# A two-layer decoder trunk on one core: every operation recorded first, then emitted in an order worked out from a table of the engines

## The chip, the core and the metric

The kernel runs on one core of a Trainium2 chip. The metric is device microseconds of one launch. A core has five engines with instruction streams of their own: TensorE (PE in the profile, its weight loads PEld), VectorE (DVE), ScalarE (ACT), GpSimd (POOL) and SyncE (SP), which here issues DMAs only; ACT issues some DMAs as well. Every engine carries out its own stream in the order in which the program was written, and waits on semaphores for the others. The question of this case is that order.

## The reference, cut to what matters

The input x has 2048 positions of 1024 features, in float32. What is computed:

```python
h = rmsnorm(x, norm_a)
b, c, xin, g = split(h @ w_in_a, 4)                    # 1024 x 4096
x = x + (b * conv3(c * xin) * silu(g)) @ w_out_a       # causal, three taps
k, v = split(rmsnorm(x, norm_kv) @ w_kv, 2)            # 8 heads of 64
q, g = split(rmsnorm(x, norm_b) @ w_in_b, 2)
for each block of 128 queries:                         # stick-breaking attention
    z = q @ k.T / 8
    rev = reversed cumulative sum over the keys of log_sigmoid(-z), strictly causal
    o = exp(z + rev) @ v
x = x + (o * silu(g)) @ w_out_b
out = rmsnorm(x, norm_f)
```

## The kernel before

**Tiling.** The 2048 positions are four chunks of 512 columns, and they are held reversed, so that the cumulative sum runs forward along the free axis and chunk c attends to chunks c, c-1, ..., 0. A product in (nearly) float32 is three matmuls in float32r: operands are split into a high and a low part (`split`, L163: a copy on ACT and a subtraction on DVE, or on POOL), and `mm3` (L192) does high x high, high x low, low x high for each of the 8 blocks of 128 input features. One output tile of 128 x 512 is therefore 24 matmuls into one bank of PSUM; the pool `lin` has two such banks.

**Stages.** `mixer_in` (L273) makes the gates C, X, B, G of the first layer for a chunk; `proj_out` (L374) its output projection; `proj_k`, `proj_q`, `proj_v`, `proj_g` (L407 to L441) the projections of the second layer; `out_b` and `out_norm` (L583, L605) the last projection and the last norm, and `out_b_last` (L623) both for chunk 3. I call all of this the filler: it is dense PE work. The other kind is `attention` (L477), by chunk and head. For a block of 128 queries (`qi`) and 512 keys it does two matmuls z (L498, L499), two sigmoids on ACT into R and w (L501, L503), on POOL a copy of the carry into R's first column, or the causal mask (L511, L507), on DVE a scan along the keys into R (L512) and the product w*R (L516); then for each 128 keys (`kb`) it transposes four blocks of w on PE into `wt` (L524), splits them into `wth` on ACT and `wtl` on DVE (L531), and adds both to `av` by two matmuls (L533, L534). Attention is what loads DVE.

**What sets the order.** Each stage is a generator that yields an estimate of its PE work. `merge` (L700) advances two or three of them in proportion to their totals (with exponents S2, S3, S4, S7 that bend the proportion), and so gives the order in which the operations are written. The framework (`schedule_with_timeline_sim`, L778) then orders them anew on each engine by a simulation of its own. In the last quarter of the program (`fine` on, L746) every third matmul of the filler has an order-only dependence on the `av` matmul of nine key blocks ago (L199 to L201), which paces the filler by the attention.

**Names that the prediction uses.** Chunk 3 is the last, with heads 3_0 to 3_7 and four blocks of keys each. `sga` is a tile of silu(g) that L556 loads over SP's queue; `gated` (L559) multiplies it with a head pair's output `ot` and splits the product into `og`, which `out_b` consumes. For the last pair `ot` is still in SBUF, and the product is L566. `pol` are the 24 matmuls (L645) that come after it. `hl` is a single buffer through which the splits of k, q and v go to DRAM.

Of the kernel before, what the change touches and what calls it, by code (L numbers as in the profile page):

```python
# [1 line left out]

# [12 lines left out]
P = 128  # L15
S = 2048
D = 1024
NH = 8
# [12 lines left out]
GRP, GRY, SLACK = 3, 6, 8  # L31
PACE = mybir.DependencyInfo(mybir.DependencyClass.NoSync, mybir.DependencyReason.DATA)
# [4 lines left out]
EPS = 1e-6  # L37

# [7 lines left out]
def kernel(  # L46
# [15 lines left out]
    nc = tc.nc  # L62

    const = ctx.enter_context(tc.tile_pool(name="const", bufs=1))
    psum = ctx.enter_context(tc.tile_pool(name="psum", bufs=2, space=bass.MemoryType.PSUM))
    dram = ctx.enter_context(tc.tile_pool(name="dram", bufs=1, space=bass.MemoryType.DRAM))
    sb = ctx.enter_context(tc.tile_pool(name="sb", bufs=2))

    ident = const.tile([P, P], F32, name="ident")
    make_identity(nc, ident)  # L70
# [23 lines left out]
    v_d = [dram.tile([P, 4, NH, 2, 64], F32, name=f"v_d_{c}") for c in range(NCH)]  # L94
    xn_d = [[dram.tile([P, 2, CH], F32, name=f"xn_d_{c}_{k}") for k in range(KD)] for c in range(NCH - 2)]
    sg_d = [[dram.tile([P, CH], F32, name=f"sg_d_{c}_{h}") for h in range(NH // 2)] for c in range(NCH)]
    og_d = [[dram.tile([P, CH], F32, name=f"og_d_{c}_{h}") for h in range(NH // 2)] for c in range(NCH)]
# [91 lines left out]
    anchors = []  # L189
    fine = [24, False]  # L190

    def mm3(ps, wts, a, kt=KD):  # L192

        hi, lo = wts[:, 0], wts[:, 1]
        n = 0
        for k in range(kt):
            for w, m in ((hi, 0), (hi, 1), (lo, 0)):
                ins = nc.tensor.matmul(ps, w[:, k, :], a[k][:, m, :], start=n == 0, stop=n == 3 * kt - 1)  # L198
# [4 lines left out]
                if n % fine[0] == 0 and n < 3 * kt:  # L203
                    yield MM * fine[0]

    def rest(n):
        return MM * (n - (n - 1) // fine[0] * fine[0])
# [219 lines left out]
    def proj_v(c, vb):  # L427
# [10 lines left out]
        nc.sync.dma_start(out=v_d[c][:, :, 2 * vb:2 * vb + 2, :, :], in_=vt.bitcast(F32))  # L438
# [38 lines left out]
    def attention(c, h, ot):  # L477
# [8 lines left out]
        for kc in range(c, -1, -1):  # L486
# [5 lines left out]
            nc.scalar.dma_start(out=vt.bitcast(F32), in_=v_d[kc][:, :, h, :, :])  # L492
# [26 lines left out]
            for kb in range(3, -1, -1):  # L519
# [14 lines left out]
                ins = nc.tensor.matmul(av[:, 0:n], vs, wl[:, 0:n], start=False, stop=final)  # L534
                anchors.append(ins)
# [47 lines left out]
    def out_b(c, obs):  # L583
# [3 lines left out]
        for ob in obs:  # L587
# [3 lines left out]
            x = ld512(f"x1o_{c}_{ob}")  # L591
# [191 lines left out]
```

## Time and profile before

| | |
|---|---|
| three runs | 1887.19, 1879.34, 1883.08 us; median 1883.08 |
| the profiled execution | 1879.53 us, of it 1877.6 us from the first to the last instruction |
| PE | 1778.2 us busy (95%), 8312 instructions |
| DVE | 1242.5 us (66%), 1830 |
| ACT, POOL | 773.3 us (41%), 432.9 us (23%) |
| DMA | 464.63 MB, mean 247 GB/s |

PE's shares are of time in which some matmul was under way; matmuls overlap in the pipe, so the mean duration of one (399 ns for a 512-wide one) is longer than the distance of two. That distance is read from a stretch in which PE never idles, as stretch over count. The clock that PE was granted is in the column PEclk (1.00 is full).

### The profile page before, as it was taken

Reading aid. Unit: us, or ns where it says so; the run is one execution under the profiler, and the core shown is the slowest. Engines: PE = TensorE matmul, PEld = TensorE weight load, DVE = VectorE, ACT = ScalarE, POOL = GpSimd, SP = SyncE. Lnnn points to the kernel's source line nnn. Section 1 sums busy time; section 2 is a strip of 40 time slices with the busy share of each in tenths; the row PEclk is TensorE's granted clock in tenths of the full one; section 3 lists DMA queues with packets and bytes.
Section 4 is the critical chain, followed back from the end, with each engine's and each line's share of the span. In section 5 each row is a group of like instructions: output and inputs, shape, how many; then the busy total and the mean of one; then the engine's idle time right before and its main releaser. Section 6 shows DMA issues by size and latency. Waiting matters only on the chain.

```text
span 1877.6 us, 24847 instructions
## 1 busy us (share of the span) xinstructions
PE 1778.2 (95%) x8312; PEld 1448.5 (77%) x8312; DVE 1242.5 (66%) x1830; ACT 773.3 (41%) x1493; POOL 432.9 (23%) x814
## 2 busy tenths in 40 slices
PE   7999999999999999999999999999998998987884
PEld 5888888888778878887888888888776886865573
DVE  7766643554243364478784477787868888799874
ACT  6423311231132142345443344454535555566542
POOL 5000000101021032032221122232223212357533
PEclk9999999999999999999999999999999999998887
DMA  9999995687978697867687765666586666878663
GB/s 295 326 297 326 330 308 168 213 311 277 337 253 285 219 324 264 286 220 250 208 253 237 257 201 187 196 200 214 186 291 202 212 205 233 275 235 261 224 203 131
DMA packets 240783, 464.63 MB, mean 247 GB/s; under 512 B 18704, under 2 KB 133392, under 8 KB 216080
## 3 DMA queue, kind: packets, MB, share of 16 engines
q1 hardware_dynamic: 180576, 404.28, 63.5%
q10 hardware_dynamic: 59920, 58.74, 11.0%
q8 instruction: 66, 1.08, 0.2%
q14 instruction: 61, 0.50, 0.1%
q0 software_dynamic: 160, 0.02, 0.1%
HBM read 326.92 MB, written 136.05 MB: 247 GB/s over the span
## 4 chain that ended last, share of the span: by engine, by line
PE 76%; DMA 9%; DVE 7%; issue 3%; ACT 2%; POOL 2%; SPq 0%; ACTq 0%; POOLq 0%; DVEq 0%
PE pG L198 9%; PE pB L198 9%; PE pX L198 9%; PE po L198 9%; PE pC L198 8%; PE pv L198 5%; PE wt L524 4%; PE pk L198 4%; PE pq L198 4%; PE pg L198 3%; PE av L534 3%; PE av L533 2%; DVE R L512 2%; PE z L498 2%; PE z L499 2%
## 5 line engine op out<-in xcount | busy, mean ns | idle before, releaser
L512 DVE TENSOR_TENSOR_SCAN R<-R,R,ones 128x512 f32<-128x512 f32 x192 | 252.5, 1317 | 32.2 <-ACT R L501 31.7
L501 ACT ACTIVATE R<-z 128x512 f32<-128x512 f32 (+1 forms) x320 | 174.2, 544 | 193.8 <-PE z L499 84.9
L165 DVE TENSOR_TENSOR wtl<-wt,wth 128x512 fp32r<-128x512 f32 (+1 forms) x320 | 186.5, 602 | 81.9 <-ACT wth L164 79.8
L164 ACT CAST wth<-wt 128x512 fp32r<-128x512 f32 (+1 forms) x320 | 160.8, 528 | 185.5 <-PE wt L524 167.4
L516 DVE TENSOR_TENSOR w<-w,R 128x512 f32<-128x512 f32 (+1 forms) x320 | 200.8, 637 | 24.9 <-POOL R L511 4.8
L198 PE MATMUL pC<-h,whl_C 128*128 128x512 f32 x768 | 191.4, 399 | 9.2 <-ACT whl_C L164 7.9
L511 POOL COPY R<-R 128x1 f32<-128x1 f32 x192 | 114.9, 599 | 346.5 <-DVE R L512 313.7
L198 PE MATMUL po<-y,whl_o 128*128 128x512 f32 x768 | 190.7, 394 | 2.7 <-DVE x L392 1.6
L198 PE MATMUL pX<-h,whl_X 128*128 128x512 f32 x768 | 188.1, 393 | 1.1 <-DVE cv L343 1.1
L198 PE MATMUL pG<-h,whl_G 128*128 128x512 f32 x768 | 185.7, 391 | 0.0
L198 PE MATMUL pB<-h,whl_B 128*128 128x512 f32 x768 | 185.6, 391 | 0.0
L524 PE MATMUL wt<-ident,w 128*128 128x128 f32 x1088 | 175.5, 276 | 7.2 <-DVE w L516 5.5
L198 PEld LDWEIGHTS pC<-h,whl_C 128*128 128x128 f32 x768 | 144.6, 191 | 43.6 <-ACT whl_C L164 7.9
L503 ACT ACTIVATE w<-z 128x512 f32<-128x512 f32 (+1 forms) x320 | 172.0, 542 | 2.8 <-PE wt L524 2.7
L198 PEld LDWEIGHTS pX<-h,whl_X 128*128 128x128 f32 x768 | 143.1, 188 | 32.3 <-DVE cv L343 1.3
L198 PEld LDWEIGHTS po<-y,whl_o 128*128 128x128 f32 x768 | 142.4, 188 | 33.2 <-DVE x L392 1.8
L198 PEld LDWEIGHTS pG<-h,whl_G 128*128 128x128 f32 x768 | 143.4, 188 | 30.2 <-issue 0.7
L198 PEld LDWEIGHTS pB<-h,whl_B 128*128 128x128 f32 x768 | 143.4, 188 | 29.8
L524 PEld LDWEIGHTS wt<-ident,w 128*128 128x128 f32 x1088 | 136.8, 142 | 35.7 <-DVE w L516 6.9
L512 DVE TENSOR_TENSOR_SCAN R<-R,ones 128x512 f32<-128x512 f32 (+3 forms) x128 | 117.2, 920 | 45.5 <-POOL R L507 39.2
L534 PE MATMUL av<-wtl,vv 128*128 128x512 f32 (+1 forms) x320 | 125.5, 395 | 19.9 <-DVE wtl L165 19.4
L498 PE MATMUL z<-kt,q 128*128 128x512 f32 (+1 forms) x320 | 128.1, 403 | 7.1 <-ACT w L503 7.0
(161 smaller groups left out, 2662.4 us busy)
## 6 DMA issues: line engine op xcount, KB each, us to landing
whl_o<-sw_o SPq DMA_DIRECT2D x24, 1024.0 KB, 5.3
kt<-k_d ACTq DMA_DIRECT2D x80, 256.0 KB, 3.7
vv<-v_d ACTq DMA_DIRECT2D x80, 256.0 KB, 4.5
whl_C<-sw_C SPq DMA_DIRECT2D x16, 1024.0 KB, 5.3
whl_X<-sw_X SPq DMA_DIRECT2D x16, 1024.0 KB, 5.0
whl_B<-sw_B SPq DMA_DIRECT2D x16, 1024.0 KB, 5.5
whl_G<-sw_G SPq DMA_DIRECT2D x16, 1024.0 KB, 5.4
whl_k<-sw_kv SPq DMA_DIRECT2D x16, 1024.0 KB, 6.7
```

Of the source, the lines that this page charges most:

```text
L164: nc.scalar.copy(hi, src)
L165: eng.tensor_sub(lo, src, hi.bitcast(F32))
L198: ins = nc.tensor.matmul(ps, w[:, k, :], a[k][:, m, :], start=n == 0, stop=n == 3 * kt - 1)
L498: nc.tensor.matmul(ps[:, lom:CH], q2[:, 0, qi * P:(qi + 1) * P], kt[:, lom:CH], start=True, stop=False)
L499: nc.tensor.matmul(ps[:, lom:CH], q2[:, 1, qi * P:(qi + 1) * P], kt[:, lom:CH], start=False, stop=True)
L501: nc.scalar.activation(R[:, lo + 1:CH + 1], ps[:, lo:CH], AF.Sigmoid, scale=-0.125)
L503: nc.scalar.activation(w[:, lo:CH], ps[:, lo:CH], AF.Sigmoid, scale=0.125)
L511: nc.gpsimd.tensor_copy(R[:, 0:1], carry[qi])
L512: nc.vector.tensor_tensor_scan(out=R[:, lo + 1:CH + 1], data0=R[:, lo + 1:CH + 1], data1=ones[:, 0:1].to_broadcast([P, CH - lo]), initial= ...
L516: nc.vector.tensor_mul(w[:, lo:CH], w[:, lo:CH], R[:, lo:CH])
L524: nc.tensor.transpose(wt[:, qi * P:(qi + 1) * P], ws[qi][:, kb * P:(kb + 1) * P], ident)
L534: ins = nc.tensor.matmul(av[:, 0:n], vs, wl[:, 0:n], start=False, stop=final)
```

## The change

Inside the kernel `nc` is now a `Recorder`. While `nc.on` is set, an engine call makes a record `Op` with its tiles' extents, its dependences on earlier records, and from `cost` a duration (`busy`) and the time to where its result can be used (`late`). Tiles of the pools are placed in memory only when they are emitted. `order` then runs a list schedule over all records: for each engine it takes the records whose dependences are done and whose buffers are free, finds the earliest time at which one could start, and among those that could start then takes the one recorded first. Records of attention (stream 0) may be taken from up to 600 places beyond the first one of their stream that is not done, all others (stream 1) up to 2400 places. `emit` writes the program in that order, with the framework's own ordering off. The pacing dependences are gone; the generators now yield every 3 matmuls (GRY) from the start; `merge` and its exponents are as before.

Four smaller edits go with it: `v_d` is one DRAM tile for each head pair rather than one for each chunk; the unnormalised output goes to a DRAM tile `x2_d` of its own rather than over `y_d`; the tile `x1o` of `out_b` comes from the pool of eight buffers `og` rather than from the five of `ld`; and the last `sga` has its place in `hl` (named `sgl`), and its load is written as its own line.

```diff
-GRP, GRY, SLACK = 3, 6, 8
-PACE = mybir.DependencyInfo(mybir.DependencyClass.NoSync, mybir.DependencyReason.DATA)
+GRY = 3
+WIN, LEAD = (600, 2400), 0
...
+    def cost(self, o, out, rest):
...
+        if kind == PE:
+            if o.name == "transpose":
+                o.busy, o.late = 0.1085, 0.36
+            else:
...
+                o.busy = (0.111 if n == 1 else 0.96 * n / 512) if full else max(0.109, 0.0135 + n / 2400)
+                o.late = o.busy + 0.26
...
+        elif kind == DVE:
+            if o.name == "tensor_tensor_scan":
+                o.busy = 0.128 + 2.09e-3 * n
...
+            else:
+                o.busy = 0.066 + 1.042e-3 * n
+            o.late = o.busy + 0.085 + SEM
...
+    def order(self, keys, window):
...
+                    t = max(o.ready, busy[e])
...
+                t0 = min(c[0] for c in cands)
+                c = min((c for c in cands if c[0] <= t0 + 1e-9), key=lambda c: c[1:3])
+                if best is None or c[0] < best[0]:
+                    best = c
...
+            cost = o.busy
+            if e == DVE and o.name != "tensor_tensor_scan" and cost > 0.3 and t < pool_until:
+                cost += 0.3 * min(cost, pool_until - t)
+            busy[e] = o.fin = t + cost
...
+            for u in o.after:
+                u.left -= 1
+                same = u.engine is o.engine and o.late is not None
+                u.ready = max(u.ready, t + cost if same else end)
...
+    def emit(self, ops):
+        for o in ops:
+            getattr(o.engine.engine, o.name)(*map(real, o.args), **{k: real(v) for k, v in o.kw.items()})
...
-                ins = nc.tensor.matmul(ps, w[:, k, :], a[k][:, m, :], start=n == 0, stop=n == 3 * kt - 1)
-                if fine[1] and len(anchors) > SLACK and n % GRP == 0:
-
-                    tc.add_manual_dep(ins.ins, anchors[-1 - SLACK].ins.name, PACE, reason="pace")
+                nc.tensor.matmul(ps, w[:, k, :], a[k][:, m, :], start=n == 0, stop=n == 3 * kt - 1)
...
-            x = ld512(f"x1o_{c}_{ob}")
+            x = sb.tile([P, CH], F32, name=f"x1o_{c}_{ob}", tag="og", bufs=KD)
...
-            nc.sync.dma_start(out=y_d[c][ob], in_=x)
+            nc.sync.dma_start(out=x2_d[c][ob], in_=x)
...
-        sg = load_sg(c, 3)
+        sg = sb.tile([P, CH], F32, name=f"sgl_{c}", tag="hl", bufs=1)
+        nc.sync.dma_start(out=sg, in_=sg_d[c][3])
...
+    ops = nc.order(lambda o: o.index - (LEAD if o.stream == 0 else 0), WIN)
+    with tc.manual_schedule():
+        nc.emit(ops)
```

The instructions are the same ones: 8252 matmuls and transposes are written to PE's stream in both programs, 1830 operations to DVE's, 870 DMAs to SP's and 225 to ACT's. What differs is where they stand. All emitted rows carry one line, L348.

**PE, chunk 3, head 3_3** (names are tile_chunk_head_keychunk_block; the number at the end is a buffer). From the last transpose into `wt_3_3_2_3` to the second matmul that uses its split, before:

```order
L524 MATMUL wt_3_3_2_3_14569<-ident_66,w_3_3_2_3_14558 128x128
L498 MATMUL z_3_3_1_3_14688<-kt_3_3_1_14638,q2_3_3_14384 128x512
L499 MATMUL z_3_3_1_3_14688<-kt_3_3_1_14638,q2_3_3_14384 128x512
L534 MATMUL av_3_3_14387<-wtl_3_3_3_0_14497,vv_3_3_3_14390 128x256
L524 MATMUL wt_3_3_2_2_14590<-ident_66,w_3_3_2_0_14522 128x128
L524 MATMUL wt_3_3_2_2_14590<-ident_66,w_3_3_2_1_14532 128x128
L524 MATMUL wt_3_3_2_2_14590<-ident_66,w_3_3_2_2_14548 128x128
L524 MATMUL wt_3_3_2_2_14590<-ident_66,w_3_3_2_3_14558 128x128
L533 MATMUL av_3_3_14387<-wth_3_3_2_3_14574,vv_3_3_2_14515 128x512
L498 MATMUL z_3_3_0_0_14819<-kt_3_3_0_14815,q2_3_3_14384 128x512
L499 MATMUL z_3_3_0_0_14819<-kt_3_3_0_14815,q2_3_3_14384 128x512
L534 MATMUL av_3_3_14387<-wtl_3_3_2_3_14575,vv_3_3_2_14515 128x512
```

And after:

```order
L348 MATMUL wt_3_3_2_3_14648<-ident_66,w_3_3_2_3_14629 128x128
L348 MATMUL wt_3_3_2_2_14660<-ident_66,w_3_3_2_3_14629 128x128
L348 MATMUL pg_0_3_14673<-xa_0_3_12632,whl_gg0_3_14302 128x512 x2
L348 MATMUL z_3_3_1_0_14703<-kt_3_3_1_14535,q2_3_3_13864 128x512 x2
L348 MATMUL av_3_3_14580<-wth_3_3_2_3_14699,vv_3_3_2_14530 128x512
L348 MATMUL pg_0_3_14673<-xa_0_4_12634,whl_gg0_3_14302 128x512 x3
L348 MATMUL av_3_3_14580<-wtl_3_3_2_3_14708,vv_3_3_2_14530 128x512
```

Before, only attention's own matmuls stand between the two, and the next transposes among them; now five matmuls of the filler `pg` and two z do, placed singly and in threes. Over chunk 3 the distance from a tile's last transpose to its second `av` matmul has shrunk: the median of the 128 is as long as 22 of the 512-wide matmuls before and 9 now (a transpose counted as half of one).

**DVE, the same head**, from the scan of the first query block of keys 1, before:

```order
L512 SCALAR_TENSOR_TENSOR R_3_3_1_0_14645<-R_3_3_1_0_14645,R_3_3_2_0_14520,ones_71 128x512
L516 TENSOR_TENSOR w_3_3_1_0_14647<-w_3_3_1_0_14647,R_3_3_1_0_14645 128x512
L447 TENSOR_TENSOR sgb_0_3_14684<-sgb_0_3_14684,pg_0_3_14614 128x512
L165 TENSOR_TENSOR wtl_3_3_3_1_14489<-wt_3_3_3_1_14485,wth_3_3_3_1_14488 128x256
L165 TENSOR_TENSOR og_0_2_14725<-ogr_0_2_14728,og_0_2_14725 128x512
L512 SCALAR_TENSOR_TENSOR R_3_3_1_1_14661<-R_3_3_1_1_14661,R_3_3_2_1_14530,ones_71 128x512
L165 TENSOR_TENSOR wtl_3_3_3_0_14497<-wt_3_3_3_0_14494,wth_3_3_3_0_14496 128x128
L516 TENSOR_TENSOR w_3_3_1_1_14663<-w_3_3_1_1_14663,R_3_3_1_1_14661 128x512
```

And after:

```order
L348 SCALAR_TENSOR_TENSOR R_3_3_1_0_14690<-R_3_3_1_0_14690,R_3_3_2_0_14520,ones_71 128x512
L348 TENSOR_TENSOR w_3_3_1_0_14717<-w_3_3_1_0_14717,R_3_3_1_0_14690 128x512
L348 TENSOR_TENSOR wtl_3_3_2_1_14748<-wt_3_3_2_1_14723,wth_3_3_2_1_14732 128x512
L348 TENSOR_TENSOR wtl_3_3_2_0_14753<-wt_3_3_2_0_14728,wth_3_3_2_0_14745 128x512
L348 SCALAR_TENSOR_TENSOR R_3_3_1_1_14738<-R_3_3_1_1_14738,R_3_3_2_1_14591,ones_71 128x512
L348 TENSOR_TENSOR w_3_3_1_1_14756<-w_3_3_1_1_14756,R_3_3_1_1_14738 128x512
L348 SCALAR_TENSOR_TENSOR R_3_3_1_2_14773<-R_3_3_1_2_14773,R_3_3_2_2_14636,ones_71 128x512
L348 TENSOR_TENSOR w_3_3_1_2_14769<-w_3_3_1_2_14769,R_3_3_1_2_14773 128x512
```

Filler (`sgb`, `og`) and splits stood between the scans; now a scan is more often followed at once by the product that needs its result: 45 of the 128 scans of chunk 3 before, 83 now (in chunks 0 to 2 together 86 of 192 before, 147 now).

**SP's queue, the last silu tile.** Before, its load stands among the stores of chunk 2's result, close to the end:

```order
L613 DMA out_0_dram<-x2r_2_4_17243 128x512
L611 DMA x2r_2_7_17255<-y_d_2_7_108 128x512
L613 DMA out_0_dram<-x2r_2_5_17247 128x512
L556 DMA sga_3_3_17429<-sg_d_3_3_232 128x512
L613 DMA out_0_dram<-x2r_2_6_17251 128x512
```

Now it stands some 180 DMAs earlier, right behind the store of what it reads:

```order
L348 DMA whl_gg0_3_14302<-sw_b7_336 128x2048
L348 DMA sg_d_3_3_244<-sgb_3_3_14300 128x512
L348 DMA sgl_3_14374<-sg_d_3_3_244 128x512
L348 DMA whl_gg1_0_14421<-sw_b4_329 128x2048
L348 DMA sg_d_0_0_229<-sgb_0_0_14419 128x512
```

**PE, where attention is crowded.** The merged order still decides how far attention and filler are when, but not everywhere. From the first z of head 1_2 (chunk 1, head 2) to the first z of head 1_6 PE's stream holds 564 instructions before, 413 of them 512 wide, and 385 now, 240 of them 512 wide; DVE's stream has 140 operations wider than four columns before and 131 now between the scans of the same heads.

More of the change, by code (lines that the diff above doesn't have):

```diff
@@ L533, in attention @@
                 nc.tensor.matmul(av[:, 0:n], vs, wh[:, 0:n], start=first, stop=False)
-                ins = nc.tensor.matmul(av[:, 0:n], vs, wl[:, 0:n], start=False, stop=final)
-                anchors.append(ins)
+                nc.tensor.matmul(av[:, 0:n], vs, wl[:, 0:n], start=False, stop=final)
                 if kb:
```

285 lines of the change are left out of this document (263 added, 22 removed).

## The prediction

> **What bounds the kernel now.** I read the page first, then the windows by stage, then who waited for whom, and last the chain at the end.
>
> ```profile
> span 1877.6 us, 24847 instructions
> PE 1778.2 (95%) x8312; PEld 1448.5 (77%) x8312; DVE 1242.5 (66%) x1830; ACT 773.3 (41%) x1493; POOL 432.9 (23%) x814
> PEclk9999999999999999999999999999999999998887
> ```
>
> PE is busy for 95% of the span, so what a new order can win is small from the start: what PE does not do usefully. The last line shows where that is: the granted clock drops in the last three slices, after long full ones. The windows divide the span by stage (in each row the span's length, then busy time and count of PE, PEld, DVE, ACT, POOL, the clock, DMA):
>
> ```profile
> core 0: us, PE busy (x) PEld busy (x) DVE busy (x) ACT busy (x) POOL busy (x), PEclk, DMA share, GB/s
> 0.00:50.00 50.00, 39.49 (x153) 28.82 (x154) 36.61 (x49) 33.91 (x53) 29.87 (x30) 1.00 1.01 294
> 50.00:500.00 450.00, 449.32 (x1990) 371.08 (x1990) 241.47 (x372) 119.96 (x174) 21.50 (x43) 1.00 0.85 288
> 500.00:710.00 210.00, 201.45 (x931) 165.53 (x930) 96.14 (x161) 58.91 (x133) 38.10 (x105) 0.98 0.82 276
> 710.00:1343.00 633.00, 631.02 (x3100) 524.48 (x3100) 443.45 (x643) 278.41 (x581) 142.38 (x342) 1.00 0.69 226
> 1343.00:1407.00 64.00, 57.68 (x275) 44.78 (x274) 44.99 (x77) 29.08 (x58) 16.97 (x25) 0.97 0.70 254
> 1407.00:1450.00 43.00, 35.30 (x167) 27.64 (x166) 32.92 (x43) 22.95 (x48) 12.63 (x25) 0.96 0.57 190
> 1450.00:1545.00 95.00, 94.87 (x486) 78.45 (x483) 82.49 (x112) 54.83 (x110) 21.62 (x52) 1.00 0.66 213
> 1545.00:1592.00 47.00, 38.83 (x194) 30.17 (x192) 41.78 (x55) 27.72 (x56) 14.29 (x30) 1.00 0.68 219
> 1592.00:1649.00 57.00, 57.00 (x288) 47.17 (x287) 44.53 (x59) 32.54 (x63) 19.10 (x30) 1.00 0.82 272
> 1649.00:1752.00 103.00, 85.09 (x393) 65.01 (x392) 96.51 (x138) 63.95 (x126) 60.38 (x76) 0.92 0.77 240
> 1752.00:1847.00 95.00, 74.80 (x322) 57.13 (x320) 66.30 (x98) 42.79 (x82) 49.73 (x54) 0.86 0.70 225
> 1847.00:1878.00 31.00, 13.31 (x34) 8.19 (x34) 15.33 (x33) 8.25 (x13) 6.30 (x5) 0.61 0.21 76
> ```
>
> From 50 to 500 us PE never idles: 450 us for 1990 matmuls is 226 ns each, the price of a 512-wide one, and no order improves it. From 710 to 1343 PE is busy for 631.0 of 633 us. The losses are the first 50 us (10.5 idle), 500 to 710 (8.6), 1343 to 1407 (6.3) and all that follows. The last quarter holds chunk 3 of the attention:
>
> ```profile
> 1030.00:1343.00 313.00, 313.00 (x1549) 260.65 (x1548) 231.35 (x317) 144.53 (x299) 75.04 (x165) 1.00 0.64 207
> 1407.00:1847.00 440.00, 385.88 (x1837) 305.58 (x1835) 364.53 (x500) 244.78 (x482) 177.75 (x265) 0.95 0.71 228
> ```
>
> Where attention and filler mix without a gap, a PE instruction costs 313/1549 = 202 ns. The 1837 of 1407 to 1847 would take 371 us at that price, and took 440: 69 us are lost, part as idle time (440 - 385.9 = 54), part at a lower clock. DVE was busy for 364.5 of the same 440. So two engines with nearly equal work, 371 and 365 us, need 440 together, because they take turns: PE is full from 1450 to 1545 and from 1592 to 1649 (DVE idle 12.5 in each), while DVE is nearly full from 1407 to 1450, 1545 to 1592 and 1649 to 1752 (idle 10.1, 5.2, 6.5). From 1752 to 1847 neither is (PE 20.2 idle, DVE 28.7). The waits and the chain at the end name single causes:
>
> ```profile
> PE av L534 <- DVE wtl L165: 19.4, 19, 2.4
> PE pol L198 <- ACT og L164: 8.9, 1, 8.9
> DVE og L165 <- ACT og L164: 6.4, 2, 5.7
> DVE ot L566 <- DMA sga<-sg_d: 6.2, 1, 6.2
> DVE khl L165 <- ACT khl L164: 12.9, 2, 11.2
> ```
> ```profile
> 1837.78 4.27 DMA out_dram<-x2r
> 1842.12 4.18 DMA sga<-sg_d
> 1846.39 0.70 DVE ot L566
> 1847.12 0.63 ACT og L164
> 1847.79 6.70 PE pol L198 x15
> ```
>
> The chain shows the clearest: the last `sga` was issued at 1842.12, behind a store that SP held back, DVE stood for 6.2 us, and `pol` with all after it began as much later.
>
> **The change part by part.** Nothing is computed less, so there is no saving of instructions; each term is a wait that goes or comes. The sum is made against the profiled execution's 1879.5 us.
>
> *The last load.* `sgl` is issued some 180 DMAs earlier. DVE's 6.2 us of waiting lies on the chain, and what is late next is `ot` itself, already done when the wait began. Gain 6.2.
>
> *The last head, 1752 to 1847.* DVE idles 28.7, of it 6.2 just counted; 22.5 are left, among them 6.4 in which `og`'s split stood at the head of DVE's stream for its copy on ACT. An order that puts an operation where its input is due removes such waits; no row says how many. Bounds 0 and 22.5; since the other engines are far from full there, I take two thirds, 15.
>
> *1343 to 1407.* At 202 ns the 275 instructions cost 55.6, so 8.4 of 64 us are lost, and one named cause is 12.9 us of DVE behind `khl`, which waits for the single buffer `hl`. The buffer stays single. Bounds 0 and 8.4; I take 6, since the filler now can be taken from farther ahead.
>
> *500 to 710.* PE idles 8.6, bounds 0 and 8.6, half: 4. The first 50 us hang on loads whose order on SP has hardly moved (the first twelve are the same): 0.
>
> *The DVE-heavy stretches* (1407 to 1450, 1545 to 1592, 1649 to 1752). PE loses 43 - 167 x 0.202 = 9.3, 47 - 194 x 0.202 = 7.8, 103 - 393 x 0.202 = 23.6, together 40.7. But DVE leaves only 10.1 + 5.2 + 6.5 = 21.8; the rest returns only if DVE work moves into the PE-full stretches (25 us of room). The merged order, which fixes the pace of heads against filler, is as before, and counted in the new order heads 3_0, 3_3 and 3_6 have 147, 172 and 167 PE instructions for the same scans, where before they had 168, 195 and 181: the pairing is no evener. Bounds 0 and 40.7; I take half of what DVE leaves, 11.
>
> *Given back: scans followed by their product.* These rows (start, duration) have both cases:
>
> ```profile
> 1577.80 1.28 DVE L512 TENSOR_TENSOR_SCAN R<-R,R,ones 128x512 f32<-128x512 f32 x1
> 1579.21 0.69 DVE L516 TENSOR_TENSOR w<-w,R 128x512 f32<-128x512 f32 x1
> 1579.82 0.68 DVE L165 TENSOR_TENSOR wtl<-wt,wth 128x512 fp32r<-128x512 f32 x1
> 1580.42 1.28 DVE L512 TENSOR_TENSOR_SCAN R<-R,R,ones 128x512 f32<-128x512 f32 x1
> 1581.61 0.67 DVE L165 TENSOR_TENSOR wtl<-wt,wth 128x512 fp32r<-128x512 f32 x1
> ```
>
> A scan followed by another tile's split is left after 1.19 us, one followed by its own product after 1.41: 0.22 more. `cost` has `u.ready = t + cost` for the same engine and does not know it. In chunk 3 there are 83 - 45 = 38 more such pairs, 8.4 us; 288 of its 440 us are DVE-heavy or in the last head, where this counts, so 5. In chunks 0 to 2 the 61 more lie beside PE's full time: 0; without that cover, 13.
>
> *Given back: less between the transposes and `av`.*
>
> ```profile
> L524 PE MATMUL wt<-ident,w 128*128 128x128 f32 x1088 | 175.5, 276 | 7.2 <-DVE w L516 5.5 <-DVE wtl L165 1.6
> L164 ACT CAST wth<-wt 128x512 fp32r<-128x512 f32 x224 | 128.2, 592 | 144.8 <-PE wt L524 134.5 <-DVE w L516 4.4 <-DVE wtl L165 2.6
> L165 DVE TENSOR_TENSOR wtl<-wt,wth 128x512 fp32r<-128x512 f32 x224 | 149.6, 682 | 61.1 <-ACT wth L164 60.7
> ```
>
> From the last transpose to the second `av` matmul PE needs 276 + 592 + 682 = 1550 ns and the hand-overs between engines (0.03 and 0.04 us in the chain above). Before, 22 matmuls (5.0 us) stood between in the median; now 9, or 2.0 us: enough when ACT and DVE are free, not when DVE has one more operation of 0.68 in front. Behind a late `av` stands all of PE, and DVE and ACT then wait for its next z. Before, `av` waited 19 times for `wtl` in the last part, 1.0 us each (19.4). Bounds: 0, and for 230 of the 320 tiles one operation less the 0.3 us of room, 0.4 x 230 = 90. I take 2: the table's durations agree with the rows (DVE 0.60 against 0.60 start to start), so the order already stands where the results arrive.
>
> *Given back: crowding.* From the first z of head 1_2 to that of 1_6, and of 2_1 to 2_3:
>
> ```profile
> 825.70:942.20 116.50, 114.52 (x571) 95.00 (x570) 96.58 (x150) 57.27 (x120) 26.26 (x72) 1.00 0.70 231
> 1093.40:1176.70 83.30, 83.30 (x418) 69.58 (x417) 65.72 (x91) 38.89 (x81) 20.81 (x50) 1.00 0.60 195
> ```
>
> PE carried 571 and 418 instructions there. In the new order the first has 385, which at 204 ns (633/3100, the row above) is 79 us, but DVE 131 of its 150 operations, so 96.6 x 131/150 = 84 to 90 us; the second 277, 56 us, against 80 of 91, 58 us. PE then idles some 11 and 2 us in a stage where it now never does, since filler that waits for DVE to empty its two PSUM banks cannot fill in. Bounds 0 and 17, half: 8.
>
> Sum: -6.2 - 15 - 6 - 4 - 11 + 5 + 2 + 8 = -27, so 1852 of this execution. It stands 3.5 below the median of the runs shown, so for a median I say 1856.
>
> *A rule beside it.* These rows are scans: the shortest, the median and the longest; and the mean in the last part:
>
> ```profile
> L512 DVE TENSOR_TENSOR_SCAN R<-R,R,ones x192: 1252/1279/2324, 764.3 to 1817.8; 128x512 f32<-128x512 f32 x192
> L512 DVE TENSOR_TENSOR_SCAN R<-R,R,ones 128x512 f32<-128x512 f32 x96 | 128.4, 1339 | 9.0 <-ACT R L501 8.7
> ```
>
> Most take 1.28 us, some 2.3, and the 96 of the last part cost 96 x (1339 - 1279) = 5.8 us more than at the median. The Trainium skill, "SBUF — State Buffer", section "SBUF: two separate sides", says that DVE and GpSimd share a port pair as an exclusive lock which the first to start holds for its whole instruction, so that a DVE operation with two SBUF inputs blocks. The longest scan agrees. By that rule the table, which exempts scans and charges 0.3 of an overlap elsewhere, is too kind to DVE whenever POOL works, and the sum would be some 6 us higher; I leave it to the rival below, as before bears the same collisions.
>
> **The rivals.**
>
> *More comes back.* PE's idle time is filled from up to 2400 records ahead, the two engines overlap freely in chunk 3, and it takes as long as its fuller engine, 371 + 8 us in place of 440. For it: both are nearly equal in work. Against it: the pace of the merge is kept. 1879.5 - 61 - 6 - 6, with the 8 of crowding: 1815 of this execution.
>
> *DVE sets chunk 3 anyway.* The DVE-heavy stretches stay as they are, the last head wins only `sga` and a few, and crowding and pairs take it back: -6 - 4 + 5 + 8 and nothing else is +3, so 1880 to 1886: no change. For it: 83% busy over the whole, 94% from 1649 to 1752. Against it: 28.7 us idle in the last head.
>
> *The order is too tight (slower).* In place: `av` behind `wtl`, in all four chunks. If DVE runs later than the table says (0.22 for each pair, the scans of up to 2.3 us), PE meets the results late and nothing can be pulled ahead, since each stream is fixed. At 0.25 us for each of 320 tiles that is 80 us against the gains of 42 and the other 13 given back: 1930; it decides from (42 - 13)/320 = 0.09 us a tile. For it: the old order had 5 us of room and lost 22 us in all before 1343. Against it: a late PE delays the next z too, which gives room back.
>
> **How the numbers follow.** The forecast has 0.42, more coming back 0.20, no change 0.13, too tight 0.25. The likeliest case's own range, as medians, is 1830 (each gain in full, DVE's 21.8 among them, less 15 given back) to 1870 (two thirds of the gains taken). The range for 8 in 10 reaches over the first rival to 1803 and half way into the last, to 1908. A measurement tells 0.5% (9.4 us) from no change. Faster by more: the forecast and the first rival, 0.62; within: 0.13; slower: 0.25.
>
> **What would show it.** Right: DVE's wait for `sga` is gone; PE busy above 80 of 95 us in the last head; 1407 to 1847 takes 415 to 430 us; PE's clock is back at 0.9 and more in the last slices but one; new idle PE time of some 10 us in chunk 1, with waits for DVE. Too tight: the waits of `av` for `wtl` and of `wt` for w number hundreds, from chunk 1 on, PE at a lower clock in the middle. No change: DVE above 90% from 1400 to 1800 and the span as it was. The forecast is wrong in its main step if chunk 3 is not shorter, or if the time before 1343 grows by more than 20 us.

## The result and the profile after

The changed kernel takes **1958.6 us** (median of 4, 1951.3 to 1960.7), the one before 1884.7 beside it: a ratio of **1.0389, 95% interval 1.0353 to 1.0426**, slower. The forecast was 1856, the range ended at 1908. The profiled execution took 1951.3 us itself, 71.8 more than the profiled one before (1879.5). The page of the changed kernel, span, busy time and granted clock:

```profile
span 1949.6 us, 24777 instructions
PE 1809.1 (93%) x8312; PEld 1432.0 (73%) x8312; DVE 1270.7 (65%) x1830; ACT 782.6 (40%) x1493; POOL 432.2 (22%) x814
PEclk9999999999999989999999999999999999899897
```

The 8312 matmuls are the same ones. The dip of the clock at the end, the last four slices of the kernel before (8, 8, 8, 7), is smaller, as forecast, though two of the last six slices still show 8. The mean clock is 0.976 for 0.978, so the clock does not explain the loss. For a fair comparison I cut both traces where the first z of a chunk, the first z of the last head and the first `pol` stand. Columns as in the prediction's windows. Before:

```profile
50.00:505.00 455.00, 454.32 (x2012) 375.21 (x2012) 241.47 (x372) 119.96 (x174) 21.50 (x43) 1.00 0.85 288
505.00:736.00 231.00, 222.45 (x1036) 183.05 (x1035) 108.10 (x181) 66.59 (x151) 43.67 (x123) 0.99 0.81 274
736.00:1032.00 296.00, 294.02 (x1436) 243.75 (x1435) 200.14 (x305) 126.78 (x265) 61.77 (x159) 1.00 0.74 242
1032.00:1407.00 375.00, 368.68 (x1812) 303.86 (x1811) 276.35 (x392) 173.02 (x356) 92.01 (x190) 1.00 0.65 216
1407.00:1752.00 345.00, 311.08 (x1517) 248.45 (x1516) 298.23 (x403) 201.99 (x402) 128.03 (x212) 0.97 0.71 229
```

After, with the first 50 us ahead, and the last head at the end:

```profile
0.00:50.00 50.00, 35.35 (x126) 24.93 (x127) 34.08 (x44) 28.04 (x44) 28.27 (x34) 0.97 0.94 272
50.00:513.00 463.00, 456.69 (x2014) 375.51 (x2013) 243.94 (x374) 125.65 (x182) 23.42 (x40) 1.00 0.85 286
513.00:754.00 241.00, 224.04 (x1042) 182.49 (x1040) 109.36 (x184) 68.39 (x153) 44.01 (x122) 0.98 0.75 253
754.00:1084.00 330.00, 311.95 (x1464) 249.59 (x1465) 204.58 (x306) 128.75 (x266) 64.98 (x159) 0.98 0.67 221
1084.00:1476.00 392.00, 376.76 (x1803) 296.59 (x1801) 280.18 (x392) 176.09 (x354) 86.83 (x190) 1.00 0.63 211
1476.00:1841.00 365.00, 330.17 (x1555) 251.30 (x1555) 312.08 (x411) 209.51 (x411) 129.63 (x214) 0.95 0.69 223
1841.00:1918.00 77.00, 61.74 (x283) 44.40 (x281) 70.89 (x90) 37.83 (x71) 48.73 (x51) 0.98 0.72 242
```

Read it per matmul: length over count. Chunk 1 went from 206 to 225 ns, chunk 2 from 207 to 217, the first seven heads of chunk 3 from 227 to 235. At the old price of each row the loss is 28 us in chunk 1 (330 - 1464 x 296/1436), 19 in chunk 2, 11 in those seven heads, 9 in chunk 0, 8 from 50 us to chunk 0 and 6 in the first 50 us (27 matmuls fewer). Only the last head gained. Most of the loss stands where the kernel before had little: in chunks 1 and 2 PE idled for 2 and 6 us, and now for 18 and 15.

What PE waits for, chosen rows, before and after (us in total, times, longest; PEld is the weight load, which also stands in front of a transpose):

```profile
PEld av L534 <- DVE wtl L165: 29.5, 28, 2.7
PEld wt L524 <- DVE w L516: 6.9, 4, 3.1
PE wt L524 <- DVE w L516: 5.5, 4, 2.7
```
```profile
PE wt L348 <- DVE w L348: 45.4, 36, 10.1
PE z L348 <- ACT w L348: 12.8, 16, 2.1
PE av L348 <- DVE wtl L348: 4.8, 10, 0.8
PE pol L348 <- ACT og L348: 2.8, 1, 2.8
PEld wt L348 <- DVE w L348: 67.6, 105, 3.0
PEld av L348 <- DVE wtl L348: 20.7, 57, 1.2
```

The place is new. Transposes that wait for the product w had cost 5.5 us in 4 waits; now it is 45.4 in 36. Where the weight load ahead stood, 6.9 in 4 became 67.6 in 105 (the two overlap, so these don't simply add). `av` behind `wtl`, the prediction's place, fell from 19.4 to 4.8 on PE and from 29.5 to 20.7 at the weight load, there in 57 waits for 28.

### The profile page after: what moved, and what is told of

It is laid out like the page before. It is cut to its first block, busy times and chain, and to the rows that moved or that the text cites. A ratio compares the mean times of both kernels' runs of the same rounds, so it can differ in the third digit from the quotient of the medians.

```text
span 1949.6 us, 24777 instructions
## 1 busy us (share of the span) xinstructions
PE 1809.1 (93%) x8312; PEld 1432.0 (73%) x8312; DVE 1270.7 (65%) x1830; ACT 782.6 (40%) x1493; POOL 432.2 (22%) x814
## 3 DMA queue, kind: packets, MB, share of 16 engines
q10 hardware_dynamic: 59920, 58.74, 10.5%
## 4 chain that ended last, share of the span: by engine, by line
PE 66%; DVE 14%; DMA 9%; issue 5%; ACT 3%; POOL 2%; ACTq 1%; SPq 1%; POOLq 0%; DVEq 0%
PE pX L348 8%; PE pB L348 8%; PE pG L348 8%; PE pC L348 8%; PE po L348 7%; DVE R L348 5%; PE av L348 5%; PE wt L348 4%; PE z L348 4%; PE pk L348 3%; PE pg L348 3%; PE pv L348 3%; DVE w L348 3%; PE pob L348 2%; PE pq L348 2%
## 5 line engine op out<-in xcount | busy, mean ns | idle before, releaser
L348 DVE TENSOR_TENSOR_SCAN R<-R,R,ones 128x512 f32<-128x512 f32 x192 | 254.1, 1324 | 17.8 <-ACT R L348 17.0
L348 DVE TENSOR_TENSOR wtl<-wt,wth 128x512 fp32r<-128x512 f32 (+1 forms) x320 | 182.3, 602 | 120.0 <-ACT wth L348 118.0
L348 ACT CAST wth<-wt 128x512 fp32r<-128x512 f32 (+1 forms) x320 | 156.0, 526 | 239.3 <-PE wt L348 225.7
L348 PE MATMUL wt<-ident,w 128*128 128x128 f32 x1088 | 197.7, 281 | 46.6 <-DVE w L348 45.4
L348 ACT ACTIVATE R<-z 128x512 f32<-128x512 f32 (+1 forms) x320 | 173.5, 542 | 158.0 <-PE z L348 97.5
L348 PE MATMUL z<-kt,q 128*128 128x512 f32 (+2 forms) x640 | 206.4, 398 | 24.8 <-ACT w L348 12.8
L348 DVE TENSOR_TENSOR w<-w,R 128x512 f32<-128x512 f32 (+1 forms) x320 | 212.1, 663 | 25.1 <-POOL w L348 0.5
L348 PEld LDWEIGHTS wt<-ident,w 128*128 128x128 f32 x1088 | 138.1, 143 | 109.3 <-DVE w L348 67.6
L348 PE MATMUL pC<-h,whl_C 128*128 128x512 f32 x768 | 201.0, 401 | 11.3 <-ACT whl_C L348 8.0
L348 PE MATMUL po<-y,whl_o 128*128 128x512 f32 x768 | 207.1, 396 | 1.1 <-POOL y L348 0.6
L348 PE MATMUL pB<-h,whl_B 128*128 128x512 f32 x768 | 197.4, 394 | 2.1 <-ACT whl_B L348 2.1
L348 PE MATMUL pX<-h,whl_X 128*128 128x512 f32 x768 | 197.7, 395 | 1.7 <-DVE whl_X L348 1.0
L348 PE MATMUL pG<-h,whl_G 128*128 128x512 f32 x768 | 196.4, 394 | 0.9 <-DVE qhl L348 0.9
L348 POOL COPY R<-R 128x1 f32<-128x1 f32 x192 | 104.3, 544 | 376.7 <-DVE R L348 352.5
L348 ACT ACTIVATE w<-z 128x512 f32<-128x512 f32 (+1 forms) x320 | 170.5, 541 | 36.7 <-PE z L348 32.6
L348 PEld LDWEIGHTS pC<-h,whl_C 128*128 128x128 f32 x768 | 144.7, 192 | 44.9 <-ACT whl_C L348 8.0
L348 PEld LDWEIGHTS po<-y,whl_o 128*128 128x128 f32 x768 | 142.3, 189 | 32.7 <-issue 1.3
L348 PEld LDWEIGHTS pX<-h,whl_X 128*128 128x128 f32 x768 | 142.5, 189 | 31.2 <-DVE whl_X L348 1.5
L348 PEld LDWEIGHTS pB<-h,whl_B 128*128 128x128 f32 x768 | 142.5, 189 | 31.2 <-ACT whl_B L348 2.9
L348 PEld LDWEIGHTS pG<-h,whl_G 128*128 128x128 f32 x768 | 142.3, 189 | 29.7 <-DVE qhl L348 1.2
L348 PEld LDWEIGHTS z<-kt,q 128*128 128x128 f32 x640 | 114.2, 194 | 54.1 <-ACT w L348 22.2
L348 DVE TENSOR_TENSOR_SCAN R<-R,ones 128x512 f32<-128x512 f32 (+3 forms) x128 | 117.2, 916 | 34.7 <-POOL R L348 34.5
```

What stands on the lines that cost most here:

```text
L348: getattr(o.engine.engine, o.name)(*map(real, o.args), **{k: real(v) for k, v in o.kw.items()})
```

## The experiments

The order comes out of a plan: the recorder gives each operation a start time and emits in that order. Plan and trace can be paired matmul by matmul, so that the time splits in two: the plan's length, and the chip's **distance** from it (start of the last matmul in the trace less its start in the plan). For the changed kernel the plan ends at 1826.8 and the distance is 117.1 us. By 500 us it is 10.7; then some 19 come in chunk 0, 20 in chunk 1, 14 in chunk 2, 38 in the first seven heads of chunk 3 and 11 in the last head. So in chunks 1 and 2 the distance covers 34 of the 47 us lost against the kernel before, and the plan itself is slower there; in the seven heads the plan was some 27 us shorter than the kernel before, and the distance took more than that. The clock is no rival for the distance: in e5_comb below it is 27.7 us at a mean clock of 0.977. Three theories on the distance: **one wrong row** (scan to own product takes 0.2 us longer than the table says), **DMA issues hold ScalarE**, and **no room** (every leg a little late, with nothing in hand).

**Order, pacing or small edits?** Three kernels under the framework's order: the changed one with the recorder off (`nc.on = True` removed, the emission too), and from the kernel before one edit each.

```diff
 e6_nopace
-                if fine[1] and len(anchors) > SLACK and n % GRP == 0:
-                    tc.add_manual_dep(ins.ins, anchors[-1 - SLACK].ins.name, PACE, reason="pace")
 e7_edits (with v_d in four pieces and x2_d as in the change)
-            x = ld512(f"x1o_{c}_{ob}")
+            x = sb.tile([P, CH], F32, name=f"x1o_{c}_{ob}", tag="og", bufs=KD)
 e7_edits and e7_sgl
-        sg = load_sg(c, 3)
+        sg = sb.tile([P, CH], F32, name=f"sgl_{c}", tag="hl", bufs=1)
+        nc.sync.dma_start(out=sg, in_=sg_d[c][3])
```

> The changed kernel with the recorder left off, so that the framework orders the work as before; the small edits (sgl early, x1o in the og buffers, x2_d, v_d in four) and the yields every 3 matmuls stay, and there are no pacing dependences. If the new order costs the 74 us: 1870 to 1895 us. If the missing pacing or one of the small edits costs them: 1930 us or more. Between the two both have a share.

> The kernel before, with the pacing dependences taken out and nothing else; the framework orders the work. The changed kernel under the framework's order took 1918, 37 us more than before. If the missing pacing is what costs these: 1905 to 1925 us. If it is the finer yields of chunks 0 to 2 or a small edit: 1875 to 1890 us.

> The kernel before, with the small edits alone (sgl loaded early into the hl buffer, x1o in the og buffers, x2_d beside y_d, v_d in four pieces); order and pacing are the framework's as before. By the prediction's term for the last load, 6 us less: 1870 to 1878 us. If a small edit is what cost the 37 us of the framework's order: 1895 us or more.

> The kernel before with the one edit of the last gate's load (sgl in the hl buffer, issued early) and nothing else. The prediction's term is 6.2 us: 1876 to 1880 us by the ratio 0.9967. All small edits together gave 0.9953; if the gain is another edit's: 0.999 to 1.001.

Measured: e4_own 1917.9, ratio 1.0195 (1.0159 to 1.0230); e6_nopace 1.0024 (1.0011 to 1.0037); e7_edits **0.9953** (0.9934 to 0.9972); e7_sgl 0.9971 (0.9952 to 0.9990). So pacing was worth only 0.24%, and the small edits gain 0.47%, of which the last gate's load alone gives 0.29%, 5.5 us. e4_own lies between the two ranges that were expected for it: half of the loss is there without the recorded order. By subtraction (1.95 - 0.24 + 0.47) some 2.2% falls to the yields every 3 matmuls under the framework's order, if the parts simply add; no run had only these.

**A control.** One constant of the table moved by 0.01 us.

```diff
-SEM = 0.09
+SEM = 0.10
```

> A control: the changed kernel with one constant of its table moved by 0.01 us (SEM 0.10 in place of 0.09). The order changes in many places, the plan's length by 0.5 us. If the gains of 22 to 30 us of the single edits come from what they say: 1950 to 1967 us, as the changed kernel. If any other order would have given them: 1940 us or less.

Measured 1949.1, just under its range, 1.0331 (1.0314 to 1.0348): the ratio moved by 0.0058, 11 us (by the two intervals, 0.0017 to 0.0099). How much of this is the reshuffled order is not shown: the profiled executions of the two took 1951.3 and 1950.5, and 1951.3 is the fastest of the changed kernel's four, 7 us under its median. Either way, differences of 10 us between two orders say little by themselves. The distance, 116.3 for 117.1, is taken from those single executions, so for the changed kernel it is the low end.

**The three theories, one edit each, and together.**

```diff
 e1_dve (in order)
-                u.ready = max(u.ready, t + cost if same else end)
+                u.ready = max(u.ready, t + cost + (0.2 if e == DVE else 0.0) if same else end)
 e2_sp (in attention: q2, kt, vv)
-            nc.scalar.dma_start(out=kt.bitcast(F32), in_=k_d[kc][h])
+            nc.sync.dma_start(out=kt.bitcast(F32), in_=k_d[kc][h])
 e3_slack (PE's two lateness constants 0.3 later as well)
-SEM = 0.09
+SEM = 0.39
```

> The changed kernel, with 0.2 us more in the table between a VectorE operation and one on VectorE that needs its result (the step scan to product stands 0.2 us longer on the chip than in the plan). The plan grows by 9 us. Theory 'one wrong row' (the products come late because the table misses this): the waits of the first transposes for w, 45 + 36 + 10 us in the group, fall under 30 and the time comes to 1890 to 1925 us. Theory 'no room' (every leg is a little late and the order keeps nothing in hand): 1945 to 1965 us. Theory 'the DMA issues hold ScalarE': 1945 to 1970 us.

> The changed kernel, with the attention's loads of q2, kt and vv issued by SP in place of ScalarE; the table's order is otherwise the same to 0.1 us in length. Theory 'the DMA issues hold ScalarE' (it stands at an issue until the transfer eight places earlier has landed, some 43 us behind these loads): the idle time of ScalarE behind DMA issues falls under 10 us and the time to 1905 to 1935 us. Theories 'one wrong row' and 'no room': 1945 to 1970 us, as the waits of the transposes for w stay.

> The changed kernel, with 0.3 us more in the table on every step from one engine to another (SEM 0.39, PE's own 0.3 later), so that the order keeps that much room; the plan grows by 31 us. Theory 'no room': the chip keeps closer to the plan and the time comes to 1890 to 1930 us. Theory 'one wrong row' (the step inside VectorE is not in this edit) and theory 'the DMA issues hold ScalarE': 1955 to 1990 us, the plan's 31 us added in part.

> The changed kernel, with the three earlier edits together: 0.2 us more between dependent VectorE operations, 0.3 us more on every step between engines, and the attention's loads issued by SP. Alone they gave 22, 25 and 30 us. If they are three causes: the sum, 77 us less, 1875 to 1895 us. If they are three ways to the same room: 1905 to 1925 us, the best of them and little more (the plan alone grows by 43 us).

| run | median us | ratio (95%) | plan us | distance us |
|---|---|---|---|---|
| changed | 1958.6 | 1.0389 (1.0353 to 1.0426) | 1826.8 | 117.1 |
| e1_dve | 1936.1 | 1.0290 (1.0252 to 1.0328) | 1836.2 | 85.3 |
| e2_sp | 1933.8 | 1.0273 (1.0241 to 1.0306) | 1826.8 | 99.2 |
| e3_slack | 1928.9 | 1.0254 (1.0217 to 1.0291) | 1858.0 | 62.0 |
| e5_comb | 1908.2 | 1.0126 (1.0106 to 1.0145) | 1869.5 | 27.7 |

Each edit beats the changed kernel. e2_sp and e3_slack came to the slow end of what their own theories had said, e1_dve fell between its theory (to 1925) and the others (from 1945). No theory had foreseen that all three edits help. Against the changed kernel the gains are 0.0099, 0.0116 and 0.0135, against the control 0.0041, 0.0058 and 0.0077; the first of these three, with an interval of about 0.004 either way, is not clear of noise. Together they give 0.0263 against the changed kernel, less than the sum of 0.0350, and e5_comb lies in the range (1905 to 1925) that was expected if the three are ways to the same room; against the control it is 0.0205, more than the sum of 0.0176. So these runs do not tell three causes from one; leaving each edit out, below, does it better. The distance shows how far each holds the chip to its plan: the VectorE row takes away 32 us (and pays 9 in the plan), the loads 18, the room 55 (and pays 31).

What the wrong row is, shown by VectorE's stream of the changed kernel in chunk 3 (start, duration):

```profile
1558.90 1.28 DVE L348 TENSOR_TENSOR_SCAN R<-R,R,ones 128x512 f32<-128x512 f32 x1
1560.31 0.69 DVE L348 TENSOR_TENSOR w<-w,R 128x512 f32<-128x512 f32 x1
1560.92 1.28 DVE L348 TENSOR_TENSOR_SCAN R<-R,R,ones 128x512 f32<-128x512 f32 x1
1562.34 0.69 DVE L348 TENSOR_TENSOR w<-w,R 128x512 f32<-128x512 f32 x1
1578.09 1.28 DVE L348 TENSOR_TENSOR_SCAN R<-R,R,ones 128x512 f32<-128x512 f32 x1
1579.29 1.13 DVE L348 TENSOR_TENSOR wtl<-wt,wth 128x512 fp32r<-128x512 f32 x2
```

Here a product follows its own scan after 1.41 us, another tile's split follows a scan after 1.20. Over the whole run, behind 512-wide scans of the usual length and with no idle time noted between, the medians are 1.39 us (139 products) and 1.20 (30 splits). It is not the kind of operation: in e1_dve the product of another tile (`w_3_2_0_1` behind the scan of `R_3_2_0_2`) starts after 1.20, and 15 such products after 1.18 in the median.

```profile
1598.66 1.29 DVE L348 TENSOR_TENSOR_SCAN R<-R,R,ones 128x512 f32<-128x512 f32 x1 [0.30 <-ACT R L348]
1599.86 0.67 DVE L348 TENSOR_TENSOR w<-w,R 128x512 f32<-128x512 f32 x1
```

In the order of the changed kernel 230 of 320 products stand right behind their scan (before: 131), in e1_dve 67. VectorE's busy time tells the same, 1270.7 us and 1251.0, and so does the product w of e1_dve, by who waited for it (us, times):

```profile
  PEld wt L348: 24.4, 33
  PE wt L348: 13.5, 21
```

The Trainium skill, "VectorE: DVE Perf Modes", section "The DRAIN you can't avoid", says that in a chain of eight copies a semaphore after each operation cost nothing extra. That does not carry over to this case's trace: the product, which waits for VectorE's own semaphore, starts 0.21 us later than an operation that does not need the one in front.

What holds ScalarE, shown at one place of the changed kernel (ACTq: DMA issues on ScalarE; in brackets the idle time before, and what ended it):

```profile
676.06 0.30 ACT L348 ACTIVATE w<-z 128x128 f32<-128x128 f32 x1
684.24 2.51 ACTq L348 DMA_DIRECT2D q<-q_d  x2
688.11 0.33 ACTq L348 DMA_DIRECT2D kt<-k_d  x1
688.47 0.58 ACT L348 COPY ot<-av 64x512 f32<-64x512 f32 x1 [12.12 <-DMA q<-q_d]
689.08 0.69 DVE L348 TENSOR_TENSOR ot<-ot,av 64x512 f32<-64x512 f32 x1 [10.48 <-ACT ot L348]
689.81 0.69 DVE L348 TENSOR_TENSOR w<-w,R 128x512 f32<-128x512 f32 x1
```

Loads that the plan counts at 0.06 us each held ScalarE for 12.1 us, VectorE stood 10.5 behind it, and the transposes 10.1: the longest wait in the list above. The reason is in ScalarE's own stream, listed with what each entry waits for:

```
DMA q2_0_6_5436<-q_d_0_3_184 64x1024 [waits DMAHW4_49,DMAHW2_49]
DMA q2_0_6_5436<-q_d_0_3_184 64x1024 [waits DMAHW4_49]
DMA kt_0_6_0_5440<-k_d_0_6_155 128x512 [waits DMAHW6_49]
```

In this program eight such semaphores serve the 1095 DMAs of SP and ScalarE in turn, so an issue waits until the transfer eight places earlier has landed. For each of these three it is a store of `xn_d` that SP had issued. The chain through this stretch names the last of them (start, length):

```profile
675.96 12.13 DMA xn_d<-xn
688.09 0.02 issue
688.11 0.33 ACTq L348
```

Over the whole run ten groups of ScalarE's waits end with a q, kt or vv load, together 44.7 us; the first, a middle and the last of them:

```profile
ACT ot L348 <- DMA q<-q_d: 12.1, 1, 12.1
...
ACT R L348 <- DMA kt<-k_d: 3.1, 1, 3.1
...
ACT vT L348 <- DMA vv<-v_d: 2.0, 1, 2.0
```

Before there was one (4.2 us), in e2_sp there is none. The Trainium skill, "DMA: Bandwidth & Descriptors", section "Anatomy of one DMA — SWDGE (gpsimd) path", says that a semaphore wait of a DMA happens on the issuing sequencer, before dispatch; this trace agrees, with 12.1 us.

**The plan itself.** Two edits change what the plan is, not its table.

```diff
 w400
-WIN, LEAD = (600, 2400), 0
+WIN, LEAD = (600, 400), 0
 grain (fine = 24 until chunk 3, then 6)
-                if n % GRY == 0 and n < 3 * kt:
-                    yield MM * GRY
+                if n % fine[0] == 0 and n < 3 * kt:
+                    yield MM * fine[0]
```

> The changed kernel, with the window of the filler stream at 400 operations in place of 2400, so that less filler runs ahead of the attention; the plan ends 17 us earlier (1809 for 1827). If what is lost stands in the plan itself (filler drawn forward, VectorE-heavy heads crowded at the end): 1930 to 1945 us. Theory 'no room' (what is lost is the distance from plan to chip, 117 us): a tighter plan is missed by more, 1945 to 1970 us.

> The changed kernel, recorded with the yields of the kernel before (24 matmuls at a time up to chunk 3, 6 from there) in place of 3 throughout; the plan ends 6.5 us earlier. Under the framework's order the fine yields, the missing pacing and the small edits came together to +37 us, of which pacing alone gave +5 and the edits alone -9, so that some 41 are left to the yields. If the recorded order works through the same thing (how finely filler is mixed into the attention): 1925 to 1945 us. If the yields only set a tie-break here: 1945 to 1960 us.

Measured: w400 1934.4, 1.0266 (1.0250 to 1.0281), plan 1809.4, distance 119.5; grain 1940.5, 1.0287 (1.0267 to 1.0306), plan 1820.3, distance 117.0. The distance is that of the changed kernel in both, so what they gain is the plan's: the profiled executions are 15 and 7 us shorter, the plans 17 and 6.5. For grain, 8 us beyond the control, the run alone decides nothing.

**All five, and each table edit left out.** e6_all is e5_comb with w400 and grain; e6_half has 0.15 us of room in place of 0.3; l1, l2 and l3 are e6_all without the VectorE row, the loads on SP, and the room.

> The three edits of the combination (1908 us) with the filler's window at 400 and the yields of the kernel before; the plan ends at 1836, 34 us earlier than the combination's 1869, with the same room in it. The combination's chip stayed within 28 us of its plan. If plan and distance add: 1870 to 1882 us, at or below the kernel before. If the shorter plan is missed by more, as in the window's run alone (17 us of plan gave 24): 1890 to 1910 us.

> The same, with half the room (0.15 us more on each step between engines in place of 0.3); the plan ends at 1825. If 0.15 us covers what the chip needs: 1865 to 1878 us, below the run with 0.3. If the room is what holds the chip to the plan: 1885 to 1910 us, above it.

> e6_all (1877 us) without the 0.2 us between dependent VectorE operations; room, loads on SP, window and yields stay. The plan's length is the same (1837). If the row for VectorE's dependent pairs is a cause of its own: 1890 us or more, and the products that follow their own scan are again above 200 of 320. If the 0.3 us of room covers it: 1873 to 1883 us.

> e6_all without the loads on SP: q2, kt and vv are issued by ScalarE again; plan 1842. If ScalarE's stand at the issues is a cause of its own: 1895 to 1910 us (its 25 us back). If the room covers it: 1878 to 1888 us.

> e6_all without the 0.3 us of room on the steps between engines; plan 1816, 20 us earlier. If the two mended causes (VectorE's row, the loads) were all that was wrong with the table: the plan's 20 us are won, 1855 to 1868 us, below both kernels. If the room is what holds the chip to the plan: 1885 to 1910 us.

| run | median us | ratio (95%) | plan us | distance us |
|---|---|---|---|---|
| e6_all | 1877.3 | 0.9951 (0.9936 to 0.9966) | 1835.7 | 34.6 |
| e6_half | 1877.7 | 0.9959 (0.9944 to 0.9974) | 1824.8 | 49.8 |
| l1_nodve | 1895.1 | 1.0058 (1.0041 to 1.0075) | 1837.2 | 51.4 |
| l2_nosp | 1890.7 | 1.0037 (1.0020 to 1.0054) | 1842.0 | 39.5 |
| l3_noroom | 1883.5 | 0.9997 (0.9979 to 1.0015) | 1815.5 | 64.2 |

The VectorE row is a cause of its own: without it 0.0107 is lost, 20 us, with the plan only 1.5 us longer, and 237 products stand behind their scans again (e6_all: 67). (The edit puts the 0.2 us between any two dependent VectorE operations, not only behind scans.) For the loads the time alone does not decide: of 0.0086 or 16 us the longer plan makes 6, what is left is no more than the control moved, and 1890.7 lies between the two expectations. But ScalarE waits behind these loads for 28.6 us again in l2_nosp (1.9 in e6_all), and e2_sp took 18 us off the distance at an equal plan, so I count them as a cause whose size is open. The room is not settled: it takes 30 us off the distance and adds 20 to the plan, and what is left, 0.0046 or 9 us, is no more than the control moved; half of it did as well. Chunks 1 and 2 and the first seven heads of chunk 3 in e6_all, and PE's waits for VectorE:

```profile
759.60:1057.20 297.60, 286.43 (x1351) 231.38 (x1351) 195.04 (x297) 123.30 (x258) 74.78 (x157) 0.98 0.68 227
1057.20:1430.70 373.50, 365.88 (x1796) 299.42 (x1794) 272.37 (x392) 176.09 (x357) 84.94 (x191) 1.00 0.62 207
1430.70:1773.10 342.40, 321.32 (x1579) 254.42 (x1580) 306.65 (x411) 208.41 (x413) 134.85 (x215) 0.99 0.79 261
```
```profile
PE wt L348 <- DVE w L348: 14.5, 17, 1.8
PE av L348 <- DVE wtl L348: 9.3, 12, 2.0
```

Chunk 2 is back at 208 ns a matmul, the heads of chunk 3 stand at 217, below both kernels; chunk 1, at 220, is not mended. PE waits for w a third as long as in the changed kernel. e6_all is 0.5% faster than the kernel before. So is e7_edits, which has the framework's order and only the small edits that e6_all has as well. So against the same edits even the mended order wins nothing over the framework's.

## Why the prediction was wrong

One step failed above all, the term for the room between transposes and `av`, and the direction with it. A second thing was in no term: what window and yields do to the plan. Of the other terms some were right and some did not come.

- *The last load, -6.2*: right. e7_sgl measured -5.5 (its interval is 1.9 to 9.0), and the wait for `sga` is gone.
- *The last head, -15 (with the load -21)*: the stage is 18 us shorter, 77 for 95, but 8 us of that is the 39 matmuls that moved out of it. At 202 ns the loss fell from 30.0 to 19.8: 10 of the 21. PE's share there did not rise, 80% for 79%, where above 80 of 95 us was forecast.
- *1343 to 1407, -6*: did not come, and a reading was wrong. The 12.9 us of DVE behind `khl` stand after 1407, none in this stretch. In the changed kernel the 275 matmuls ahead of chunk 3 take some 67 us, for 64.
- *Crowding, +8*: the two stages came as forecast, though what they cost the whole was not measured by itself. Heads 1_2 to 1_5 were forecast at 84 to 90 us with 11 of PE idle, heads 2_1 to 2_2 at 58 with 2 (the third row is chunk 3, for the next point):

```profile
836.90:925.30 88.40, 78.06 (x389) 60.35 (x387) 79.09 (x115) 49.84 (x109) 29.27 (x73) 1.00 0.58 178
1137.60:1193.80 56.20, 54.18 (x278) 42.47 (x278) 54.37 (x75) 36.35 (x76) 18.96 (x43) 1.00 0.51 164
1476.30:1918.40 442.10, 391.75 (x1834) 295.70 (x1834) 383.03 (x500) 247.65 (x483) 178.36 (x264) 0.96 0.70 226
```

- *500 to 710, -4, and the DVE-heavy stretches of chunk 3, -11*: neither came. Chunk 3 took 442.1 us (last row) for 440; 415 to 430 was the sign for it. What the last head won, the seven before it lost.
- *Scans followed by their product, +5*: the mechanism was right, the size was not. The 38 pairs more in chunk 3 were priced in part, the 61 in chunks 0 to 2 at nothing, since PE was full beside them. In the changed kernel it was not: PE idles 18 and 15 us in chunks 1 and 2. All 99 at 0.22 us would be 22 us. The 20 us that leaving the row out of e6_all cost go with 170 pairs, not 99, so not every pair costs its full price, and what the 99 cost is open.
- *Less room between transposes and `av`, +2*: **here the prediction failed.** It said: "the table's durations agree with the rows (DVE 0.60 against 0.60 start to start), so the order already stands where the results arrive". The durations do agree. The hand-overs do not: the step behind a scan, the DMA issues and, not measured one by one, some lateness on the other legs. This order puts each operation where its input is due, so such lateness comes into PE's stream and adds up: 117 us of distance, where 15 had been given back. Without the distance the profiled execution would have been at 1951.3 - 117.1 = 1834, below even the 1852 of the sum: the sum had priced the plan and left out what the chip makes of it. (No run came closer to its plan than 27.7 us, so 1834 is a bound, not a time that was within reach.) The three edits of the hand-overs together won back 0.0263, some 50 us.
- *The rival "too tight"* had the right sign, and its price of a DVE later than the table is what happened. Its sum had the wrong join: what grew is the waits of `wt` for w, not of `av` for `wtl`. Its signs came in part: `wt` for w 36 times on PE and 105 at the weight load, `av` for `wtl` only 10 and 57, the clock in chunk 1 at 0.98 for 1.00. Its 1930 was 21 us below the profiled execution; ScalarE's stands behind DMA issues were in no case.
- *The first 50 us, 0*: 27 matmuls fewer in them, some 6 us; the order on SP had been looked at for its first twelve entries alone.
- *The shared lock* that the Trainium skill, "SBUF — State Buffer", section "SBUF: two separate sides", tells of, beside the sum: by it 6 us more were named. The longest scans agree with it: each kernel has 11 scans of 512 columns that took over 1.5 us, all beside work of GpSimd. But the 192 scans of this form took only 1.6 us more in all:

```profile
L512 DVE TENSOR_TENSOR_SCAN R<-R,R,ones 128x512 f32<-128x512 f32 x192 | 252.5, 1317 | 32.2 <-ACT R L501 31.7
```
```profile
L348 DVE TENSOR_TENSOR_SCAN R<-R,R,ones 128x512 f32<-128x512 f32 x192 | 254.1, 1324 | 17.8 <-ACT R L348 17.0
```

From the changed kernel to e6_all the ratio falls by 0.0438, 82 us. By the runs 33 are window and yields (e5_comb to e6_all, whose plans differ by 34 us); no term of the prediction held these, though by the subtraction above the yields cost some 41 us under the framework's order. The three other edits, each by leaving it out, make 20, 16 (6 of it plan) and 9; 4 are left over. Beyond the plan the last two are no more than what the control moved.

## What to carry to other kernels

This order, fixed from a table, failed at the hand-overs and not at the durations. So pair the plan with the trace, operation by operation, and look at the distance first, since it tells a bad plan from a good plan that the chip can't keep. Ask of every operation that is costed at nothing because another engine is full whether that engine stays full under the new order. And change one constant of the table by a hair before believing a gain of 10 us: the control moved by as much here.

## What the runs showed of the hardware

A VectorE operation that needs the result of the one in front starts 0.21 us later than one that does not (1.41 us against 1.20 behind the same 512-wide scan, also for the same kind of operation). A load issued by ScalarE can hold the engine for as long as an unrelated store needs: 12.1 us here, since this program's eight completion semaphores are handed out in turn over both issuing engines.
